# The gate and retention-value projections of a hybrid decoder block as twelve pairs of blocks in seven parts each, with h sums and gates kept in DRAM

## The chip, the cores and the metric

The kernel runs on one core of one Trainium2 chip. The metric is the device time of one execution in microseconds (us); less is better. Three runs of the kernel before gave a median of 1450.76 us (1450.04 to 1456.05).

## The reference, cut to what is computed

One decoder block for 1024 positions of width 1024, in float32. h is the RMS-normalised input; one matrix `w_in` projects it to everything the two branches need.

```python
h = rms_norm(x, g_mix)
q1, q2, k1, k2, va, qr, kr, vr, gr, gate_a, gate_r = split(h @ w_in)
a = diff_attention(q1, q2, k1, k2, va, lam)        # 4 heads, causal, ALiBi
a = _rms(a) * g_diff_sub * (1 - lam_init)
r = _rms(retention(qr, kr, vr)) * silu(gr)         # 4 heads, 8 chunks of 128 positions
merged = sigmoid(gate_a) * (a @ w_diff_proj) + sigmoid(gate_r) * (r @ w_ret_proj)
x = x + merged @ w_out
z = causal_dwconv(rms_norm(x, g_ffn) @ w_up)       # then silu(zg) * zu, @ w_down, a last RMS norm
```

The projections that the change rewrites are gr (512 columns of `w_in`), gate_a and gate_r (1024 each) and vr (512): 24 column blocks of 128.

## The kernel before, in words

Every fp32 product is made of three float32r matmuls: each operand is split into a high part (an ACT copy, `hi`) and a rest (a DVE subtraction, `lo`), and the kernel sums hi x hi, hi x lo and lo x hi (`product`, L200; `split`, L161; `weight`, L183). h lies transposed in SBUF as `hT`, eight pairs of 128x1024 tiles (tags `h0`, `h1`). SBUF tiles come from tags with a fixed number of slots (`BUFS`, L38), so a new tile waits until the slot's former tile is no longer read. PSUM has four tags, `g`, `x`, `b` and `r`, of two banks each while the branches run (L267).

The first part of `hybrid_block` runs, in the order of the text: va; normalisation of h; then for each of four heads `queries_keys` (L393: two `gemm` calls of 48 matmuls each) and `attention` (L417: eight query blocks, scores in bank `x`, an Exp, transposes in `b`, the product in `r`). After the last head come `retention_queries_keys` (L470, qr and kr) and `retention_gate` (L485, gr). `branch` (L510) scales and transposes the attention output into `aT`; `row_major` (L363) makes vr, with positions on the partitions, in matmuls of 256 columns. The retention loop (L547) works on chunk after chunk: scores `pst`, output `por`, transposed keys `pk`, state update `pu`. `gated` (L602) makes one gate block by a `gemm` over h (48 matmuls of 512 columns), a Sigmoid, and the projection of a branch (24 matmuls); it runs eight times for ga with the attention branch (`pspa`) and eight times for gt with the retention branch (`pspr`), with `branch` on the retention output between them.

The order of instructions in this part is fixed at build time by a planner, which goes by the priority of the text and by its own estimates of durations; each engine then executes its list in order. DMAs are issued from SP's queue, in a list of its own. The later part (`wo`, `up`, `wd`) is written differently: `seven_parts` (L796) and `up_step` (L986) compute products of 2x2 blocks in seven block products in place of eight (parts 1 to 7, with sums and differences of blocks), each a step of 12 matmuls per bank; `issue` (L713) emits the steps by hand, loads nine steps ahead, sums four, high parts three and rests two, under a manual schedule that keeps the text's order on PE, DVE, ACT and POOL.

## Time and profile before

| what | us |
|---|---|
| median of 3 runs | 1450.76 |
| lowest, highest | 1450.04, 1456.05 |
| the profiled execution, its own time | 1455.26 |
| its span, first to last instruction | 1453.5 |
| PE busy in it | 1393.8 (96%) |
| DVE busy | 969.0 (67%) |
| ACT busy | 658.9 (45%) |
| POOL busy | 171.6 (12%) |

Stages of the profiled execution, in us from the start of its span: normalisation and va to 68; attention with the products of q, k, qr, kr and the first gr blocks to 321; vr (316 to 368), retention (344 to 473) and ga with the attention branch (396 to 550); gt with the retention branch to 682; wo to 770; up to 1223; wd to 1440. A busy share says how long an engine had an instruction in work; whether its work set the end is read from who waited for whom in a stage.

### The profile page before, as it was taken

What the parts mean: (1) busy time and instruction counts of PE and PEld (TensorE: products, weight loads), DVE (VectorE), ACT (ScalarE), POOL (GpSimd) and SP (SyncE); (2) the same over time, 40 slices, a digit from 0 to 9 for tenths busy, and PEclk for the clock granted to TensorE, in tenths of its full rate; (3) what the DMA queues carried; (4) which work ended last, traced back from release to release, by engine and by line L of the source; (5) the groups of instructions that cost most, each with busy time, mean ns of one, the idle gap of its engine ahead of it and who ended that gap; (6) DMA issues with size and microseconds to landing.
All of it is one profiled execution on the core that took longest, in us unless ns stands there. A gap on an engine that the chain in (4) does not pass through costs nothing.

```text
span 1453.5 us, 18160 instructions
## 1 busy us (share of the span) xinstructions
PE 1393.8 (96%) x6776; PEld 1168.4 (80%) x6776; DVE 969.0 (67%) x1499; ACT 658.9 (45%) x1222; POOL 171.6 (12%) x127
## 2 busy tenths in 40 slices
PE   6899999999999999999988789999999999999996
PEld 6888888899888888888866468888888888788885
DVE  6746775552333315334978878988888899797876
ACT  6536565473222212113454355555555556454452
POOL 6621011000000000000000001111111112200000
PEclk9999999999999999999999889999999999999998
DMA  6310101000101111115224224433344365953233
GB/s 240 115 58 30 30 16 44 30 30 30 44 23 44 44 44 44 58 58 191 96 87 140 60 87 138 138 127 126 132 138 138 123 205 184 328 175 115 88 94 116
DMA packets 60472, 145.60 MB, mean 100 GB/s; under 512 B 6720, under 2 KB 9152, under 8 KB 60384
## 3 DMA queue, kind: packets, MB, share of 16 engines
q1 hardware_dynamic: 60192, 143.79, 29.8%
q8 instruction: 53, 0.87, 0.2%
q0 software_dynamic: 192, 0.66, 0.1%
q14 instruction: 35, 0.29, 0.1%
HBM read 115.84 MB, written 28.57 MB: 99 GB/s over the span
## 4 chain that ended last, share of the span: by engine, by line
PE 82%; DVE 8%; ACT 3%; issue 2%; DMA 2%; POOL 2%; SPq 0%; DVEq 0%; ACTq 0%; POOLq 0%
PE up L657 26%; PE wd L657 11%; PE psga L206 6%; PE psgt L206 6%; PE wo L657 4%; PE ps_vr L206 3%; PE psgr L206 3%; PE pspa L206 3%; PE pspr L206 3%; PE psk L206 3%; PE psq L206 3%; PE pss L431 2%; PE po L459 2%; PE pskr L206 2%; PE psqr L206 2%
## 5 line engine op out<-in xcount | busy, mean ns | idle before, releaser
L657 PE MATMUL up<-f,wf 128*128 128x512 f32 x1848 | 432.6, 395 | 18.2 <-ACT f L670 9.0
L657 PEld LDWEIGHTS up<-f,wf 128*128 128x128 f32 x1848 | 350.3, 190 | 99.9 <-ACT f L670 12.5
L657 PE MATMUL wd<-awd,wwd 128*128 128x512 f32 (+1 forms) x960 | 211.5, 382 | 2.1 <-DVE awd L664 2.1
L657 PEld LDWEIGHTS wd<-awd,wwd 128*128 128x128 f32 x960 | 175.3, 188 | 37.6 <-DVE awd L664 2.5
L657 PE MATMUL wo<-awo,wwo 128*128 128x512 f32 x336 | 80.8, 399 | 5.2 <-DVE awo L664 4.9
L657 PEld LDWEIGHTS wo<-awo,wwo 128*128 128x128 f32 x336 | 63.6, 191 | 21.7 <-DVE awo L664 7.3
L206 PE MATMUL psga<-hT,hi_ga 128*128 128x512 f32 x256 | 79.1, 391 | 0.3 <-ACT merged L605 0.3
L206 PE MATMUL psgt<-hT,hi_gt 128*128 128x512 f32 x256 | 78.1, 390 | 0.0
L1090 DVE SCALAR_TENSOR_TENSOR y<-zg,par,y 128x1022 f32<-128x1022 f32 (+1 forms) x44 | 58.6, 1333 | 5.0 <-ACT y L1087 5.0
L441 ACT ACTIVATE s<-s,row 128x512 f32<-128x512 f32 (+7 forms) x64 | 49.4, 773 | 23.4 <-DVE row L436 22.8
L664 POOL TENSOR_TENSOR t12g<-y 128x512 f32<-128x512 f32 x11 | 19.2, 1746 | 315.9 <-DVE y L1100 183.9
L667 DVE TENSOR_TENSOR zg<-zg,up 128x512 f32<-128x512 f32 x44 | 30.2, 686 | 39.2 <-PE up L657 38.4
L206 PEld LDWEIGHTS psga<-hT,hi_ga 128*128 128x128 f32 x256 | 48.0, 188 | 10.3 <-ACT merged L605 0.6
L1090 DVE SCALAR_TENSOR_TENSOR y<-zu,par,y 128x1022 f32<-128x1022 f32 (+1 forms) x44 | 56.1, 1276 | 0.0
L206 PEld LDWEIGHTS psgt<-hT,hi_gt 128*128 128x128 f32 x256 | 48.0, 188 | 9.8
L436 DVE CUSTOM_DVE_ANT_0 s<-pss,dist_t 128x512 f32<-128x512 f32 (+3 forms) x64 | 36.9, 588 | 27.0 <-PE pss L431 25.0
L670 ACT ACTIVATE zg<-up 128x512 f32<-128x512 f32 x44 | 26.3, 597 | 62.8 <-PE up L657 62.8
L664 DVE TENSOR_TENSOR awd<-act_in,awd 128x512 fp32r<-128x512 f32 x77 | 53.7, 697 | 0.0
L431 PE MATMUL pss<-k,q 128*128 128x512 f32 (+2 forms) x192 | 50.4, 370 | 2.4 <-DVE row L436 2.3
L206 PE MATMUL psga<-hT,lo_ga 128*128 128x512 f32 x128 | 50.2, 397 | 0.0
L164 DVE TENSOR_TENSOR lo_gt<-raw_gt,hi_gt 128x1024 fp32r<-128x1024 f32 x8 | 9.8, 1226 | 59.5 <-ACT hi_gt L163 59.5
L206 PE MATMUL psgt<-hT,lo_gt 128*128 128x512 f32 x128 | 48.8, 390 | 0.0
(311 smaller groups left out, 2814.9 us busy)
## 6 DMA issues: line engine op xcount, KB each, us to landing
act_in<-act SPq DMA_DIRECT2D x77, 256.0 KB, 2.9
act<-y SPq DMA_DIRECT2D x55, 256.0 KB, 2.1
raw_zg<-in_wall SPq DMA_DIRECT2D x22, 512.0 KB, 3.6
raw_zu<-in_wall SPq DMA_DIRECT2D x22, 512.0 KB, 4.2
x<-in_x SPq DMA_DIRECT2D x15, 512.0 KB, 8.4
act<-t12g SPq DMA_DIRECT2D x22, 256.0 KB, 2.0
wdu<-in_wall SPq DMA_DIRECT2D x22, 256.0 KB, 5.2
wdv<-in_wall SPq DMA_DIRECT2D x22, 256.0 KB, 4.7
```

The costliest lines, as they stand in the source:

```text
L164: engine.tensor_tensor(lo, src, hi.bitcast(F32), op=ALU.subtract)
L206: nc.tensor.matmul(ps, w, a, start=i == 0, stop=i == n - 1)
L431: nc.tensor.matmul(ps[:, : max(n, 256)], qs[m][:, i * P : (i + 1) * P], k[:, c : c + max(n, 256)], start=e == 0, stop=e == 1,)
L436: nc.vector.tensor_tensor_reduce(s[:, c : c + n], ps[:, :n], dst_t[:, S - width + c : S - width + c + n], SLOPES[h], low_, op0=ALU.add, op ...
L441: nc.scalar.activation(s[:, :width], s[:, :width], AF.Exp, bias=low_, scale=-1.0, accum_out=z[:, m : m + 1])
L459: nc.tensor.matmul(po, at[:, k * P : (k + 1) * P], va[h][:, kb, :], start=kb == 0, stop=kb == i)
L657: nc.tensor.matmul(ps[:, cols], w[:, x + at : x + at + P], a[:, y + cols.start : y + cols.stop], start=start and i == 0, stop=stop and i = ...
L664: engine.tensor_tensor(out, a, b, op=ALU.subtract)
L667: engine.tensor_tensor(out, a, b, op=ALU.add)
L670: nc.scalar.activation(out, a, AF.Copy)
L1090: nc.vector.scalar_tensor_tensor(y[side][:, n:], z[:, : S - n], t[:, j : j + 1], y[side][:, n:], op0=ALU.mult, op1=ALU.add)
```

## The change

- Columns of gr, ga, gt and vr are taken as 12 pairs of blocks. With the two halves of the positions and the two halves of the width a pair is a 2x2 block product, made in seven parts of 12 matmuls of 512 columns (`Pair`, on the `Step` and `issue` machinery that moves up from the later part).
- Sums of blocks of h (`h_sums`) are made on DVE in the middle of the attention stage and stored in DRAM; `h_side` loads them back in halves and splits them for parts 4 to 7. Part 5's lie over the second half of `hT[0..3]`.
- vr is made with columns on the partitions like the other pairs and transposed chunk by chunk.
- qr, kr (`retention_product`) and the finished gates go to DRAM (`spill`) and are loaded back when used (`loaded`). The decay of q is a DVE multiplication after the reload.
- The last head's attention is cut in three pieces with higher priority; steps 0 to 3 of the pairs stand between the pieces, all others after `branch` for the attention output.
- Retention runs after all pairs, with the inputs of chunk c+1 (`chunk_inputs`) ahead of chunk c, and the projection of the attention branch (`pspa`) follows it in the text.

```diff
-    for p in range(2):
-        halves(("vr", p), w_in, O_VR + p * 256)
+    for i in range(NH):
+        add(("vr", i), _unit_columns(w_in, np.arange(O_VR + i * P, O_VR + (i + 1) * P)))
...
+    def part(ps, ws, acts, start, stop, cols=slice(0, 512)):
+        n = 3 * len(ws)
+        i = 0
+        for (w, at), a in zip(ws, acts):
+            for x, y in ((0, 0), (0, 1), (1, 0)):
+                nc.tensor.matmul(
+                    ps[:, cols], w[:, x * 512 + at : x * 512 + at + P], a[y][:, cols],
+                    start=start and i == 0, stop=stop and i == n - 1, skip_group_check=True,
...
+    def issue(first=-LOAD, end=None):
+        n = len(steps)
+        for i in range(first, n if end is None else end):
+            for ahead, ops in (
+                (0, lambda s: s.first), (LOAD, lambda s: s.load), (SUMS, lambda s: s.sums), (HI, lambda s: [f.hi for f in s.forms]),
+                (LO, lambda s: [f.lo for f in s.forms]), (0, lambda s: s.pre + [s.mm] + s.post),
+            ):
...
+    def manual():
+        return tc.manual_schedule(engines={getattr(mybir.EngineType, n) for n in ("PE", "DVE", "Activation", "Pool")})
...
-        def row_major(name, dst, tags):
...
-        def attention(h, qs, ks):
-            oa.append(t4("vo", f"oa{h}", shape=(P, NST, DV)))
-            for i in (3, 7, 6, 5, 4, 2, 1, 0):
+        def attention(h, qs, ks, blocks=(3, 7, 6, 5, 4, 2, 1, 0)):
+            if len(oa) == h:
+                oa.append(t4("vo", f"oa{h}", shape=(P, NST, DV)))
...
-        def retention_queries_keys(p):
...
-        def retention_gate(h):
...
+        def spill(name, i, t):
+            spilled[name, i] = dram.tile([P, S], F32, name=f"{name}_saved{i}")
+            nc.sync.dma_start(out=spilled[name, i], in_=t)
+        def loaded(name, i, tag):
+            t = t4(tag, f"{name}{i}_in")
+            queue.last = nc.sync.dma_start(out=t, in_=spilled[name, i]).ins
+            return t
+        def retention_product(name, p):
+            t = t4("br", f"{name}{p}")
+            gemm((name, p), "g", f"{name}{p}", lambda cs, ps: copy(t[:, cs], ps), nc.gpsimd)
+            spill(name, p, t)
...
+        def h_sums():
+            for k in range(HK):
+                a, b = t4("vo", f"ta{k}"), t4("br", f"tb{k}")
+                for t, e in ((a, k), (b, k + HK)):
+                    plus(t, hT[0][e].bitcast(F32), hT[1][e].bitcast(F32))
+                b11, b12, b21, b22 = a[:, 0:512], a[:, 512:], b[:, 0:512], b[:, 512:]
+                sub(b11, b12, b11)
+                sub(b12, b22, b12)
+                sub(b22, b22, b11)
+                sub(b21, b21, b22)
+                t_saved.append([dram.tile([P, S], F32, name=f"t_saved{e}_{k}") for e in range(2)])
+                for t, d in zip((a, b), t_saved[k]):
+                    nc.sync.dma_start(out=d, in_=t)
+        h_sides = {(p, k): [t[k + q][:, cs] for t in hT] for p, q, cs in ((1, 0, first_half), (2, HK, first_half), (3, HK, second_half)) for k in range(HK)}
+        def h_side(p, k, tag=None):
+            if tag:
+                t = t4(tag, f"ht{p}_{k}", F32R)
+                hi, lo = t[:, 0:512], t[:, 512:]
+            else:
+                hi, lo = (t[k][:, second_half] for t in hT)
+            e, cs = {5: (0, first_half), 7: (0, second_half), 4: (1, first_half), 6: (1, second_half)}[p]
+            nc.sync.dma_start(out=lo.bitcast(F32), in_=t_saved[k][e][:, cs])
+            split(lo.bitcast(F32), hi, lo)
+            h_sides[p, k] = hi, lo
...
+        class Pair:
+            def __init__(self, i, name, e, func, done):
+                self.i, self.names, self.func, self.done = i, ((name, e), (name, e + 1)), func, done
+                self.label = f"{name}{e}"
+                self.tags = ("wraw", "wraw") if i % 2 == 0 else ("vo", "g")
+            def load(self, q):
+                t = t4(self.tags[q], f"raw{q}_{self.label}")
+                queue.load_unit(t, self.names[q])
+                if q == 0:
+                    self.a11, self.a12 = t[:, 0:512], t[:, 512:]
+                else:
+                    self.a21, self.a22 = t[:, 0:512], t[:, 512:]
...
+            def add(self, p):
+                side = {1: "a11", 2: "a12", 5: "a21", 6: "s2", 7: "a11", 3: "a12", 4: "a22"}[p]
+                w = weight_form(lambda: getattr(self, side), f"w{self.label}_{p}")
+                into_a = p in (1, 6, 7, 4)
+                def mm():
+                    if p == 1:
+                        self.a = psum("g", f"pa_{self.label}")
+                    if p in (2, 5):
+                        self.b = psum("x", f"pb{p}_{self.label}")
+                    part(
+                        self.a if into_a else self.b, [(w.t, k * P) for k in range(HK)],
+                        [h_sides[p, k] for k in range(HK)], p in (1, 2, 5), True,
+                    )
+                load, sums, post = [], [], []
+                if p == 1:
+                    load.append(partial(self.load, 0))
...
+                    def sums_5():
+                        sub(self.a11, self.a11, self.a21)
+                        self.s2 = t4("at", f"s2_{self.label}", shape=(P, 512))
+                        sub(self.s2, self.a22, self.a11)
+                        plus(self.a21, self.a21, self.a22)
...
+        for i, p in ((0, 1), (0, 2), (1, 1), (1, 2), (0, 5), (0, 6), (0, 3), (0, 7), (1, 5), (0, 4)):
+            pairs[i].add(p)
+        for i in range(1, len(pairs)):
+            for e, p in ((0, 6), (1, 1), (0, 3), (0, 7), (1, 2), (0, 4), (1, 5)):
+                if i + e < len(pairs):
+                    pairs[i + e].add(p)
         qk = queries_keys(0)
-        for h in range(NH):
+        for h in range(NH - 1):
             attention(h, *qk)
-            if h + 1 < NH:
-                qk = queries_keys(h + 1)
-            else:
-                for p in range(2):
-                    retention_queries_keys(p)
-                for e in range(2):
-                    retention_gate(e)
+            qk = queries_keys(h + 1)
+            if h == 1:
+                h_sums()
+        attention(3, *qk, (3, 7, 6))
+        level = tc.cur_priority
+        for name in ("qr", "kr"):
+            for p in range(2):
+                retention_product(name, p)
+        for k in range(HK):
+            h_side(5, k)
+        for p, tag in ((6, "br"), (7, "br")):
+            for k in range(HK):
+                h_side(p, k, tag)
+        def urgent():
+            return tc.high_priority(tc.cur_priority - level)
+        with urgent():
+            attention(3, *qk, (5, 4))
+        with manual():
+            issue(end=2)
+        with urgent():
+            attention(3, *qk, (2, 1, 0))
+        with manual():
+            issue(2, 4)
+        for k, tag in enumerate(("br", "c", "c", "c")):
+            h_side(4, k, tag)
         gd = one.tile([P, 1], F32, name="gd")
         nc.vector.tensor_scalar(gd, par[:, PAR_SUB : PAR_SUB + 1], 1.0 - LAM_INIT, None, op0=ALU.mult)
...
-        vr = [t4("vo", f"vr{i}", shape=(P, 2, 512)) for i in range(4)]
-        aT = branch(oa, ssq_a, lambda h, st: oa[h][:, st, :], "a", ("c", "c", "br", "s"), finish_a)
+        aT = branch(
+            oa, ssq_a, lambda h, st: oa[h][:, st, :], "a", (("vo", "c"), ("vo", "s"), ("vo", "s"), ("vo", "vo")), finish_a
+        )
+        with manual():
+            issue(4)
+        merged = [None] * KB
+        MERGED = ("br",) * 5 + ("s", "s", "vo")
+        merged[0] = loaded("ga", 0, MERGED[0])
+        rq, rk = ([loaded(name, p, "h1") for p in range(2)] for name in ("qr", "kr"))
         for p in range(2):
-            row_major(("vr", p), lambda st: vr[st // 2][:, st % 2, p * 256 : (p + 1) * 256], "gx")
+            q = rq[p].rearrange("p (c s) -> p c s", c=NST)
+            nc.vector.tensor_tensor(q, q, qd_c[:, p].broadcast_to([P, NST, P]), op=ALU.mult)
+        for j in range(1, 5):
+            merged[j] = loaded("ga", j, MERGED[j])
+        sgr = [loaded("gr", h, "h0") for h in range(NH)]
+        vr = []
         orr = []
         ssq_r = one.tile([P, NST * NH], F32, name="ssq_r")
-        state = None
         qz = t4("g", "qz", shape=(P, 2, 2, 2, P))
         nc.gpsimd.memset(qz, 0.0)
-        for c in range(NST):
+        heads = [(h, h // 2, slice((h % 2) * HD, (h % 2 + 1) * HD), slice(h * DV, (h + 1) * DV)) for h in range(NH)]
+        ready = {}
+        def chunk_inputs(c):
             cs = slice(c * P, (c + 1) * P)
             q = qz[:, c % 2]
             for p in range(2):
                 for e, rows in ((0, low), (1, top)):
                     nc.gpsimd.tensor_copy(q[rows, p, e, :], rq[p][rows, cs])
+            pv = psum("b", f"pv{c}")
+            for i in range(NH):
+                nc.tensor.transpose(pv[:, i * P : (i + 1) * P], vT[i][:, cs], ident)
+            if c % 2 == 0:
+                vr.append(t4("br", f"vr{c}", shape=(P, 2, 512)))
             v = vr[c // 2][:, c % 2, :]
-            heads = [(h, h // 2, slice((h % 2) * HD, (h % 2 + 1) * HD), slice(h * DV, (h + 1) * DV)) for h in range(NH)]
+            copy(v, pv)
             pst = psum("r", f"pst{c}")
             for p in range(2):
                 nc.tensor.matmul(
...
+            kd = None
+            if c + 1 < NST:
+                pk = psum("b", f"pk{c}")[:, 0:256]
+                for p in range(2):
+                    nc.tensor.transpose(pk[:, p * P : (p + 1) * P], rk[p][:, cs], ident)
+                kd = t4("kd", f"kd{c}", shape=(P, 256))
+                nc.vector.tensor_tensor(
+                    kd.rearrange("p (h d) -> p h d", h=NH), pk.rearrange("p (h d) -> p h d", h=NH),
+                    kd_c.broadcast_to([P, NH, HD]), op=ALU.mult,
+                )
+            ready[c] = q, v, sc, kd
...
+        def chunk(c, state):
+            q, v, sc, kd = ready.pop(c)
+            new = None
+            if kd is not None:
+                pu = psum("r", f"pu{c}")
+                for p in range(2):
+                    vs = slice(p * 256, (p + 1) * 256)
+                    nc.tensor.matmul(pu[:, vs], kd[:, p * P : (p + 1) * P], v[:, vs], start=True, stop=True)
+                new = t4("st", f"state{c}", shape=(P, 2, DV))
+                for h, p, rows, hs in heads:
+                    if c:
+                        nc.vector.scalar_tensor_tensor(
+                            new[rows, p, :], state[rows, p, :], math.exp(float(LOG_G[h]) * P), pu[rows, hs], op0=ALU.mult, op1=ALU.add
+                        )
+                    else:
+                        nc.vector.tensor_copy(new[rows, p, :], pu[rows, hs])
             po = psum("r", f"por{c}")
             for h, p, rows, hs in heads:
...
-            for h, p, rows, hs in heads:
-                if c:
-                    nc.vector.scalar_tensor_tensor(
-                        new[rows, p, :], state[rows, p, :], math.exp(float(LOG_G[h]) * P), pu[rows, hs], op0=ALU.mult, op1=ALU.add
-                    )
-                else:
-                    nc.vector.tensor_copy(new[rows, p, :], pu[rows, hs])
-            state = new
-        for h in range(2, NH):
-            retention_gate(h)
...
-        def gated(j, names, b, g):
-            gemm((names[0], j), "gx", f"{names[0]}{j}", lambda cs, ps: nc.scalar.activation(g[:, cs], ps, AF.Sigmoid))
-            w = weight((names[1], j))
+            return new
+        state = None
+        chunk_inputs(0)
+        for c in range(NST):
+            if c + 1 < NST:
+                chunk_inputs(c + 1)
+            state = chunk(c, state)
+        def gated(j, name, b, g):
+            w = weight((name, j))
             for c in range(2):
                 cs = slice(c * 512, (c + 1) * 512)
-                ps = psum("gx", f"ps{names[1]}{j}_{c}")
+                ps = psum("gx", f"ps{name}{j}_{c}")
                 channel_major(ps, w, lambda k: b[k], NH, c)
                 nc.vector.tensor_tensor(g[:, cs], g[:, cs], ps, op=ALU.mult)
-        merged = [t4("br" if j < 5 else "s" if j < 7 else "vo", f"merged{j}") for j in range(KB)]
-        for j in range(KB):
-            gated(j, ("ga", "pa"), aT, merged[j])
+        for j in (0, 1, 2, 3, 4, 7, 5, 6):
+            if merged[j] is None:
+                merged[j] = loaded("ga", j, MERGED[j])
+            gated(j, "pa", aT, merged[j])
...
-        rT = branch(orr, ssq_r, lambda h, st: orr[st // 2][:, st % 2 * NH + h, :], "r", ("c", "c", "br", "br"), finish_r)
-        HK = KB // 2
+        rT = branch(orr, ssq_r, lambda h, st: orr[st // 2][:, st % 2 * NH + h, :], "r", ("cc", "cc", ("br", "br"), ("br", "br")), finish_r)
         t12 = []
         for j in (0, 4, 1, 5, 2, 6, 3, 7):
-            g = t4("s", f"gr{j}")
-            gated(j, ("gt", "pr"), rT, g)
+            g = loaded("gt", j, "s")
+            gated(j, "pr", rT, g)
             nc.vector.tensor_tensor(merged[j], merged[j], g, op=ALU.add)
             if j >= HK:
                 b11, b12, b22 = merged[j - HK][:, 0:512], merged[j - HK][:, 512:], merged[j][:, 512:]
```

## Rows read from the trace of the kernel before

**Rows 1.** The page's head and its first part: span; engine, busy us (share of the span), instructions.

```profile
span 1453.5 us, 18160 instructions
PE 1393.8 (96%) x6776; PEld 1168.4 (80%) x6776; DVE 969.0 (67%) x1499; ACT 658.9 (45%) x1222; POOL 171.6 (12%) x127
```

**Rows 2.** Busy time by stage: stretch, its length, busy us and instructions of each engine, granted clock of PE, busy share of the DMA engines, GB/s.

```profile
94.80:285.00 190.20, 186.61 (x1020) 160.08 (x1019) 122.35 (x322) 108.80 (x256) 22.35 (x9) 0.99 0.09 29
285.00:321.30 36.30, 36.30 (x217) 32.07 (x216) 18.38 (x51) 25.23 (x51) 3.31 (x9) 1.00 0.14 43
...
396.00:473.00 77.00, 76.66 (x394) 65.55 (x392) 25.45 (x49) 16.43 (x55) 5.08 (x16) 1.00 0.12 35
...
550.00:682.00 132.00, 132.00 (x593) 109.38 (x592) 47.55 (x62) 28.95 (x44) 5.32 (x3) 1.00 0.20 66
```

**Rows 3.** What PE waited for from 60 to 690 us: us in total, times, longest.

```profile
PE pss L431 <- DVE row L436: 2.3, 3, 1.2
PE psq L206 <- POOL lo_q L164: 2.1, 1, 2.1
```

**Rows 4.** Groups of PE instructions from 280 to 700 us: count | busy us, mean ns of one | idle before. The mean is a latency, since matmuls overlap. A weight's high part takes part in two of the three matmuls of a product and its rest in one, so a lo row has half the count of its hi row.

```profile
L206 PE MATMUL psga<-hT,hi_ga 128*128 128x512 f32 x256 | 79.1, 391 | 0.3 <-ACT merged L605 0.3
L206 PE MATMUL psgt<-hT,hi_gt 128*128 128x512 f32 x256 | 78.1, 390 | 0.0
L206 PE MATMUL psga<-hT,lo_ga 128*128 128x512 f32 x128 | 50.2, 397 | 0.0
...
L206 PE MATMUL ps_vr<-hi_vr,hT 128*128 128x256 f32 x256 | 47.6, 285 | 0.0
L206 PE MATMUL psgr<-hT,hi_gr 128*128 128x512 f32 x128 | 40.2, 393 | 0.0
L206 PE MATMUL pspa<-a,hi_pa 128*128 128x512 f32 x128 | 39.9, 391 | 0.0
...
L206 PE MATMUL ps_vr<-lo_vr,hT 128*128 128x256 f32 x128 | 36.2, 285 | 0.0
```

**Rows 5.** The chain of work in order of time: start, us, instructions in an unbroken run.

```profile
344.96 23.03 PE ps_vr L206 x192
...
584.63 10.88 PE psgt L206 x48
```

**Rows 6.** PE in order of time: start, us to the end of the last, instructions.

```profile
326.68 1.04 PE L526 MATMUL pta<-cst,oa 128*128 128x128 f32 x8
327.47 0.48 PE L206 MATMUL ps_vr<-hi_vr,hT 128*128 128x256 f32 x2
```

**Rows 7.** Groups of DVE and ACT instructions from 60 to 800 us, shapes apart: count | busy us, mean ns of one | idle before.

```profile
L164 DVE TENSOR_TENSOR lo_ga<-raw_ga,hi_ga 128x1024 fp32r<-128x1024 f32 x8 | 9.8, 1225 | 43.5 <-ACT hi_ga L163 43.5
L163 ACT ACTIVATE hi_ga<-raw_ga 128x1024 fp32r<-128x1024 f32 x8 | 8.5, 1061 | 31.8 <-PE psga L206 25.9 <-PE psgr L206 5.9
L664 DVE TENSOR_TENSOR awo<-merged,awo 128x512 fp32r<-128x512 f32 x16 | 10.9, 682 | 0.0
L667 DVE TENSOR_TENSOR x<-x,wo 128x512 f32<-128x512 f32 x24 | 16.3, 684 | 9.3 <-PE wo L657 9.3
L670 ACT ACTIVATE awo<-merged 128x512 fp32r<-128x512 f32 x16 | 9.9, 617 | 0.0
L605 ACT ACTIVATE gr<-psgt 128x512 f32<-128x512 f32 x16 | 9.4, 589 | 40.8 <-PE psgt L206 40.8
```

**Rows 8.** The same view as rows 2, for the up stage.

```profile
873.00:1222.00 349.00, 348.31 (x1537) 288.07 (x1537) 310.64 (x352) 187.94 (x280) 65.49 (x39) 1.00 0.43 142
```

**Rows 9.** DMA issues: tile, queue, count, KB each, median us from issue to landing.

```profile
raw_ga<-in_wall SPq DMA_DIRECT2D x8, 512.0 KB, 3.3
...
x_saved<-x SPq DMA_DIRECT2D x16, 256.0 KB, 2.0
```

**Rows 10.** The retention loop: all its `por` matmuls of one kind (first and last start), and one chunk in order of time (start, us, engine, instructions).

```profile
L564 PE MATMUL por<-vr,rs x64: 270/275/276, 367.8 to 472.7; 128*128 128x128 f32 x64
...
428.51 0.38 PE L564 MATMUL por<-vr,rs 128*128 128x128 f32 x2
...
430.29 0.38 PE L578 MATMUL pk<-cst,rk 128*128 128x128 f32 x2
...
436.89 1.02 PE L587 MATMUL pu<-vr,kd 128*128 128x256 f32 x4
437.75 1.03 PE L557 MATMUL pst<-qz,rk 128*128 128x256 f32 x4
...
440.22 0.38 PE L564 MATMUL por<-vr,rs 128*128 128x128 f32 x2
...
444.06 0.42 DVE L580 TENSOR_TENSOR kd<-pk,cst 128x256 f32<-128x256 f32 x1
...
448.75 1.02 PE L587 MATMUL pu<-vr,kd 128*128 128x256 f32 x4
```

**Rows 11.** Groups of DVE and ACT instructions from 60 to 800 us, on the way from the last retention chunk to the retention branch's operand: count | busy us, mean ns of one | idle before.

```profile
L573 ACT ACTIVATE jkr<-or 128x128 f32<-128x128 f32 x32 | 9.5, 299 | 26.1 <-DVE or L570 26.1
L573 ACT ACTIVATION_READ_ACCUMULATOR jkr<-or 128x1 f32 x32 | 6.0, 188 | 0.0
L518 DVE TENSOR_TENSOR or<-or,rstd_r 128x1024 f32<-128x1024 f32 x4 | 4.6, 1219 | 0.0
L619 DVE TENSOR_TENSOR y<-ptr,sgr 128x512 f32<-128x512 f32 x8 | 5.3, 684 | 5.3 <-PE ptr L526 5.3
```

**Rows 12.** The same view as rows 2, for the stretch with the longest holes of PE.

```profile
800.00:840.00 40.00, 28.08 (x85) 18.83 (x85) 31.39 (x50) 15.89 (x28) 0.00 (x0) 0.79 0.18 53
```

More of the change, by code (lines that the diff above doesn't have):

```diff
@@ new lines, in hybrid_block, with weight_form, __init__, step @@
+    n_forms = [0]
+    def weight_form(src, name):
+        n_forms[0] += 1
+        return Form(("whi", "wlo")[n_forms[0] % 2], src, name)
+    class Step:
+        def __init__(self, label, mm, load=(), sums=(), forms=(), post=()):
+            self.label, self.mm, self.load, self.sums, self.forms = label, mm, list(load), list(sums), list(forms)
+            self.first, self.pre, self.post = [], [], list(post)
+    LOAD, SUMS, HI, LO = 9, 4, 3, 2
+    steps, index, behind = [], {}, []
+    def step(label, *args, **kwargs):
+        index[label] = len(steps)
+        steps.append(Step(label, *args, **kwargs))
@@ new lines, in spread @@
+    def spread(first, last, ops):
+        i, j = (index[x] if isinstance(x, tuple) else x for x in (first, last))
+        for n, op in enumerate(ops):
+            steps[i + n * (j + 1 - i) // len(ops)].post.append(op)
+    def issue(first=-LOAD, end=None):
[5 more added lines that the diff above has]
+            ):
+                if 0 <= i + ahead < n:
+                    for op in ops(steps[i + ahead]):
+                        op()
@@ L707, in spread @@
-    def spread(first, last, ops):
-        i, j = (index[x] if isinstance(x, tuple) else x for x in (first, last))
-        for n, op in enumerate(ops):
-            steps[i + n * (j + 1 - i) // len(ops)].post.append(op)
-    def issue():
-        n = len(steps)
-        for i in range(-LOAD, n):
-            for ahead, ops in (
-                (0, lambda s: s.first), (LOAD, lambda s: s.load), (SUMS, lambda s: s.sums), (HI, lambda s: [f.hi for f in s.forms]),
-                (LO, lambda s: [f.lo for f in s.forms]), (0, lambda s: s.pre + [s.mm] + s.post),
-            ):
-                if 0 <= i + ahead < n:
-                    for op in ops(steps[i + ahead]):
-                        op()
@@ L1260, in hybrid_block @@
     at(("wd", 4, "d", 1, 3), row0, column1, *rest0, row1, *rest1)
-    with tc.manual_schedule(engines={getattr(mybir.EngineType, n) for n in ("PE", "DVE", "Activation", "Pool")}):
+    with manual():
         issue()
```

172 lines of the change are left out of this document (82 added, 90 removed).

## The prediction

> **What bounds the kernel now.** I read the busy shares first: PE is busy for 1393.8 of 1453.5 us, DVE for 969.0 [rows 1]. A share over the whole span hides stages, so I cut the span by stage next. Wherever the change works PE has almost no hole: 186.6 of 190.2 us in the attention stage, all of 36.3, 76.7 of 77.0, all of 132.0, at a granted clock of 0.99 to 1.00, while DVE is busy for at most 64% of any of these [rows 2]. The list of what PE waited for between 60 and 690 us confirms it: the largest entry is 2.3 us [rows 3]. So in this region time falls only if PE has less to do, and rises if PE finds something not ready.
>
> **Matmuls.** Removed: ga 256 + 128, gt as many, gr half as many, 960 matmuls of 512 columns; vr 256 + 128, 384 of 256 columns [rows 4]. The chain gives paces, which the means do not, since those are latencies: 48 in 10.88 us, 0.2267 each; 192 of the narrow kind in 23.03 us, 0.120 each [rows 5]. So 960 x 0.2267 = 217.6 and 384 x 0.120 = 46.1, together 263.7 us. Added: 12 pairs x 7 parts x 12 = 1008 x 0.2267 = 228.5 us. vr now comes with columns on the partitions and needs 32 transposes; eight transposes hold PE from 326.68 to 327.47, 0.10 each [rows 6], so 3.2 us. Net on PE: 263.7 - 228.5 - 3.2 = 32.0 us less, on the path.
>
> The Trainium skill (TensorE: Matmul & The Clock Gate, section Back-to-back issue gap) gives a warm spacing of N / 2.4 GHz plus 2.5 ns, 216 ns at 512 columns and 109 ns at 256. By it the first difference would be an estimated 31.4 instead of 35.2 us; the rows are slower, most so for the narrow matmuls, and the sum goes by the rows.
>
> **Operands of the pairs.** A pair needs seven rests (DVE 0.682), four sums of weight blocks and three additions from PSUM (0.684 each): 14 x 0.683 = 9.6 us of DVE. ACT has seven high parts (0.617), three copies from PSUM (0.589), a function over 1024 columns (nearest row 1.061) and two over 512 (0.589): 8.3 us [rows 7]. PE works 84 x 0.2267 = 19.04 us on a pair, so both hide. The up stage is the same machinery with more on DVE, 310.6 of 349.0 us, and PE is busy for 348.3 of them [rows 8]. Steady pairs: 1 us of holes, between 0 and 4. POOL gets nothing new; its rests of q, k, qr and kr stay.
>
> **h sums and sides.** Per k two additions over 1024 columns (1.225) and four over 512 (0.684): 5.2, four times 20.7 us of DVE [rows 7] in a stage where DVE is free for 68 of 190 us [rows 2]. The 16 sides cost 16 x 0.617 = 9.9 us of ACT and 16 x 0.682 = 10.9 us of DVE, mostly late in that stage. Attention has the higher priority there, so I count nothing on the path; if DVE had no room they would cost their 20.7 us.
>
> **DMAs.** 72 more on SP's queue: 8 stores of sums, 16 half loads, 24 spills, 24 reloads, about 34 MB, on 9 to 15% busy DMA engines [rows 2]. A load of 512 KB lands in 3.3 us, a store of 256 KB in 2.0 [rows 9]. A spill waits for ACT's last pass over its block, and the next weight loads queue behind it; but a load is issued nine steps, 9 x 2.72 = 24.5 us, ahead, so the queue may slip by several landings. Nothing on the path.
>
> **Start of the pairs.** Attention needs other work in PE's gaps. Before, after q, k, qr and kr this was gr: 96 matmuls, 21.8 us. Now steps 0 to 3 give 48 matmuls, 10.9 us, and steps 4 and 5 another 5.4 if part 5's sides are there, which are written over hT after the last qr and kr product. Then a second wait: pair 1's second tile takes the one slot of tag `g`, which holds the distance table until the last score. The load (3.3), three sums (2.1) and a form (1.3) make 6.7 us, and on DVE the rests of the next steps stand behind those sums in the text's order. The hole is 0 if steps 4 and 5 and the transposes of `aT` (32, 3.2 us) cover it, and 10.9 + 6.7 = 17.6 us if nothing does. I take 5: nearer to nothing, as PE waited 2.3 us for scores in the whole stage [rows 3], so the planned order had slack.
>
> **Retention and the attention branch.** Before, retention had ga beside it and was never short of cover. Now there is `pspa` alone: 128 + 64 matmuls [rows 4], 43.5 us. Of its own work a chunk has eight output matmuls (428.51 to 430.29, 1.8 us), state update and scores (0.86 each, the distance of their starts), two key transposes and four new ones (0.6): 4.1 us [rows 6, 10]. So PE has 8 x 4.1 + 43.5 = 76.3 us, and 3.2 us of transposes for the retention branch. A chunk took 11.7 us from output to output (428.51 to 440.22), 4.3 of them between the end of `kd` and `pu`, which nothing needed [rows 10]: the plan was stretched because other work was there. With the next chunk's inputs ahead, scores, keys and `kd` leave the chain, so a chunk lies between 4.1 and 11.7 us; I take 7.5, as the part of the old chain that stays is about half of it. Behind the last chunk come a copy of about 0.7, four squares (0.299 + 0.188 each, 2.0), root and reciprocal (an estimated 2), scalings (2 x 1.22 for the first piece), a transpose, and eight pieces of 0.684 + 0.682: some 19 us to the last piece, 9 to the first [rows 7, 11]. The chain is 8 x 7.5 + 19 = 79 against 79.5 us of PE work. Not all of the cover will fall where it is wanted: I take a hole of 5 us, from 0 to 20.
>
> **Reloads and wo.** q and k of retention come back into slots that free some 10 us before the last step, four loads of 3.3 us: 1 us, up to 5. The retention projection runs without gt's products, so behind the last slot of `wraw` wo's weights have two projections, 48 matmuls and 10.9 us, in place of a gate and a projection, 16.3: 2 us, up to 6.
>
> **Sum.** 32.0 - (1 + 5 + 5 + 1 + 2) = 18 us. The profiled execution took 1455.3 us, 1.8 more than its span [rows 1], and would take 1437; it lies 4.5 above the median of the runs, so I put the median at 1450.8 - 18 = 1433 us. A measurement of this kernel can tell about 0.5%, 7.3 us, from no change.
>
> **Rivals.**
> - All hidden (chance 0.20): every hole near zero, as PE had none before; there were also 3.6 us of holes in the attention stage to lose. 1417 to 1424 us. For it: the free shares of DVE and ACT [rows 2]. Against: the cover shrinks at two places.
> - Holes dearer than their length (0.11). From 800 to 840 us PE was idle for 11.9 us, the granted clock fell to 0.79 (part of the time at 1.2 GHz), and 85 matmuls were done, 19.3 us at 0.2267: 20.7 us lost for 11.9 of holes, 1.74 times [rows 12]. My 14 us would then cost 24 and the gain be 8: 1443 us. Against: short scattered holes left the clock at 0.99 [rows 2]. The Trainium skill (TensorE: Matmul & The Clock Gate, Part 1) says that the throttled clock is the default and activity lifts it; the rows agree.
> - No gain (0.09): sums and sides crowd DVE in the attention stage, so that its scores come late: 20.7 us beside the 9 of the other holes, 32 - 30 = 2: 1449 us. For it: slots of `vo` and `br` are scarce there. Against: 68 us of DVE were free.
> - Slower (0.08): retention keeps its old step. It decides from T = 11.4 us per chunk: the hole is 8 T + 19 - 79.5, and 32 - 9 + 7.3 = 30.3 of it make the kernel 0.5% slower. At the 11.7 seen it is 33 us: 1461 us; at the mean of old starts, (472.7 - 367.8) / 7 = 15.0, it is 59.5: 1487 us [rows 10]. For it: the planner's order may again be far looser than the durations. Against: the inputs come one chunk ahead, and the planner stretched only where it had cover.
>
> The forecast has the remaining 0.52, from 1424 to 1442 us.
>
> **Numbers.** Faster: 0.52 less 0.02 for its edge, 0.20, and half of the dear holes, 0.06, with 0.02 of the third: 0.78. Slower 0.08; within 0.5% the other 0.14. The range reaches from all hidden, 1417, to the no-gain case with its edge, 1450; it leaves out the slower case and little else.
>
> **What would show it.** Right: some 84 matmuls per 19 us over 11 pairs with PE never idle; the retention branch's operand ready less than 5 us after the last `pspa`; wo starting 15 to 20 us earlier than 682. Wrong: PE waits for a side, for `raw` of pair 1 or for pair forms (start); PE idle for over 10 us between the last chunk and the first `pspr` (retention); `pss` waiting for DVE in heads 2 and 3 (sums); a granted clock under 0.95 between 300 and 680 us. If the region from 95 to 660 is dense and the gain still misses, the pace of the pairs was not 0.2267.

## The result and the profile after

The changed kernel took 1470.7 us (median; 1468.3 to 1476.1) beside 1450.6 for the kernel before: ratio 1.0135, 95% interval 1.0098 to 1.0173. It is slower by 20 us where 18 less were forecast; the range ended at 1450. The profiled execution took 1469.6 us. The page of the changed kernel, to be held against [rows 1]:

```profile
span 1467.7 us, 18058 instructions
...
PE 1380.4 (94%) x6472; PEld 1140.4 (78%) x6472; DVE 1067.6 (73%) x1673; ACT 702.4 (48%) x1312; POOL 175.8 (12%) x127
```

PE does less, as planned, and yet the span is longer: it must idle, or run slowly, somewhere. The windows of the changed kernel (columns as in [rows 2]) say where. First the whole region of the change, then the steady pairs, `wo`, `up`, `wd`, then seven slices of 10 us:

```profile
60.00:690.00 630.00, 592.49 (x2890) 492.12 (x2889) 367.45 (x729) 276.34 (x599) 54.17 (x54) 0.96 0.26 91
...
360.00:540.00 180.00, 180.00 (x796) 148.99 (x795) 85.90 (x133) 75.73 (x124) 0.00 (x0) 1.00 0.33 110
698.00:786.00 88.00, 81.14 (x345) 64.53 (x344) 74.61 (x119) 42.66 (x79) 6.50 (x1) 0.98 0.34 122
786.00:1239.00 453.00, 434.80 (x1858) 352.81 (x1859) 392.88 (x472) 237.96 (x365) 67.71 (x40) 0.97 0.39 130
1239.00:1454.00 215.00, 212.91 (x976) 177.04 (x974) 173.82 (x275) 102.86 (x186) 10.25 (x4) 1.00 0.47 159
...
180.00:190.00 10.00, 6.09 (x20) 3.85 (x21) 10.00 (x21) 3.88 (x9) 2.59 (x1) 0.71 0.44 159
190.00:200.00 10.00, 7.27 (x47) 6.01 (x46) 10.00 (x30) 6.32 (x20) 0.00 (x0) 0.95 0.26 106
200.00:210.00 10.00, 7.53 (x29) 6.30 (x30) 8.20 (x22) 3.94 (x13) 0.00 (x0) 0.66 0.26 105
330.00:340.00 10.00, 2.27 (x10) 1.79 (x10) 7.77 (x12) 3.67 (x8) 0.00 (x0) 0.72 0.16 52
340.00:350.00 10.00, 8.88 (x34) 6.95 (x34) 4.51 (x7) 5.25 (x10) 0.00 (x0) 0.59 0.01 2
...
630.00:640.00 10.00, 7.20 (x53) 6.13 (x51) 3.91 (x8) 3.58 (x21) 1.17 (x4) 1.00 0.01 4
640.00:650.00 10.00, 4.75 (x16) 2.94 (x17) 7.54 (x10) 3.48 (x9) 0.00 (x0) 0.58 0.00 1
```

From 60 to 690 us PE idles 37.5 of 630 us; by the same view it idled 7.8 in the kernel before, at a clock of 0.99. The pairs are dense, and the later stages last as long as before: `wo` starts at 697.5 in place of 682.4 us, and the end is later by about as much. So the loss lies ahead of `wo`, mostly in three holes: 176 to 210 (A), 329 to 350 (B), 623 to 650 us (C). What PE waited for in the changed kernel (us in total, times, longest), beside [rows 3]:

```profile
PE pss L502 <- DVE row L507: 9.2, 10, 2.3
PE ptr L754 <- DVE or L746: 6.8, 4, 5.4
PE pta L754 <- DVE oa L746: 5.7, 1, 5.7
PE pat L525 <- DVE s L517: 3.9, 4, 1.9
PE pta L754 <- DVE a L762: 2.7, 2, 2.0
...
PE por L841 <- DVE state L834: 2.1, 2, 1.2
```

Every line names VectorE, none a transfer (VectorE and ScalarE themselves waited 1.0 to 1.5 us for transfers at 323 to 327 us, while PE had work). Each hole in order of time (start, us, engine, instruction, idle before).

**Hole A.** The h sums (`ta`, `tb`) stand between the attention's VectorE instructions. One of them took 2.31 us, where the same form took 0.68 at 192.25, beside a GpSimd instruction, and PE's longest wait for scores (2.33 us) ends behind it. The q evictions of head 3 start at 200.65 us (174.21 in the kernel before), so bank `g` is full and no q or k matmul can fill:

```profile
180.15 2.59 POOL L164 TENSOR_TENSOR lo_qr<-raw_qr,hi_qr 128x1024 fp32r<-128x1024 f32 x1 [14.09 <-ACT hi_qr L163]
180.97 2.31 DVE L285 TENSOR_TENSOR tb<-tb,ta 128x512 f32<-128x512 f32 x1
183.94 3.03 PE L502 MATMUL pss<-k,q 128*128 128x512 f32 x6 [2.33 <-DVE row L507]
...
185.62 1.22 DVE L288 TENSOR_TENSOR ta<-hT,hT 128x1024 f32<-128x1024 f32 x1
...
186.76 1.14 DVE L517 SCALAR_TENSOR_TENSOR s<-s,row,s 128x896 f32<-128x896 f32 x1
...
188.04 1.73 PE L525 MATMUL pat<-cst,s 128*128 128x128 f32 x7 [1.07 <-DVE s L517]
...
200.65 0.69 DVE L472 SCALAR_TENSOR_TENSOR q<-psq,q 64x512 fp32r<-64x512 f32 x1
...
202.40 1.30 PE L525 MATMUL pat<-cst,s 128*128 128x128 f32 x5 [1.89 <-DVE s L517]
...
206.42 1.20 PE L206 MATMUL psk<-hT,hi_k 128*128 128x512 f32 x2
```

**Hole B.** After the last output of attention PE's list has the branch's transposes (`pta`) ahead of the next pair step, and PE waits there 5.70 us for the branch's scale; a copy of the pairs (`z_gr`, 0.59 us) stands on ScalarE behind five evictions of the branch, and the next pair step needs its bank. The first line is the first sum from the tile in slot `g` that the prediction named:

```profile
326.00 0.69 DVE L285 TENSOR_TENSOR raw_gr<-raw_gr,raw_gr 128x512 f32<-128x512 f32 x1 [1.52 <-DMA raw_gr<-in_wall]
...
329.28 0.83 PE L530 MATMUL po<-va,at 128*128 128x128 f32 x6
...
334.44 4.63 DVE L746 TENSOR_TENSOR oa<-oa,rstd_a 128x1024 f32<-128x1024 f32 x4
335.81 1.94 PE L754 MATMUL pta<-cst,oa 128*128 128x128 f32 x8 [5.70 <-DVE oa L746]
...
343.61 0.69 ACT L761 ACTIVATE a<-pta,gd 128x512 fp32r<-128x512 f32 x1 [1.14 <-PE pta L754]
344.20 0.59 ACT L291 ACTIVATE z_gr<-pb_gr 128x512 f32<-128x512 f32 x1
...
344.84 4.53 PE L276 MATMUL pb_gr<-hT,wgr 128*128 128x512 f32 x12 [0.41 <-ACT z_gr L291]
```

**Hole C.** `pspa` starts at 558.1 us, 16 us ahead of the first output of retention (574.1), and its last matmul at 626.1, while the last chunk's outputs run to 638.5. Behind them stands the chain to the retention operand, with nothing to cover it:

```profile
638.09 0.39 PE L843 MATMUL por<-state,qz 128*128 128x128 f32 x2
...
638.52 0.69 DVE L847 COPY or<-por 128x512 f32<-128x512 f32 x1 [1.09 <-PE por L843]
...
640.60 1.28 ACT L742 ACT_TABLE_LOAD   x1
...
642.63 4.63 DVE L746 TENSOR_TENSOR or<-or,rstd_r 128x1024 f32<-128x1024 f32 x4
643.91 0.69 PE L754 MATMUL ptr<-cst,or 128*128 128x128 f32 x2 [5.44 <-DVE or L746]
...
648.69 1.20 PE L206 MATMUL pspr<-r,hi_pr 128*128 128x512 f32 x2
```

**The account** of the two profiled executions. The changed kernel starts `wo` 15.1 us later, though its first q product comes 3.0 us earlier (65.9 in place of 68.9 us): in the first 60 us the kernel before lost 3.0 us to a lower clock (0.94), the changed one none. So the stretch from the first q product to `wo` takes 18.1 us longer. In it stand 32.0 us less work, 36.7 - 6.1 = 30.6 more idle time, and 13.0 more from the clock (PE's busy time x (1 - granted clock), summed over slices of 1 us from 60 us on: 16.2 against 3.2). That makes +11.6; 6.5 us were not found in rows. By place, more than in the kernel before (idle + clock): hole A, 170 to 220 us, 7.9 + 3.8; hole B with the stretch ahead of it, 280 to 360, 13.3 + 4.6; hole C, 625 to 670, 9.3 + 3.3.

### The profile page after: what moved, and what is told of

Same layout as the page of the kernel before. It is cut to its first block, busy times and chain, and to the rows that moved or that the text cites. A ratio compares the mean times of both kernels' runs of the same rounds, so it can differ in the third digit from the quotient of the medians.

```text
span 1467.7 us, 18058 instructions
## 1 busy us (share of the span) xinstructions
PE 1380.4 (94%) x6472; PEld 1140.4 (78%) x6472; DVE 1067.6 (73%) x1673; ACT 702.4 (48%) x1312; POOL 175.8 (12%) x127
## 4 chain that ended last, share of the span: by engine, by line
PE 79%; DVE 10%; ACT 4%; issue 2%; POOL 2%; DMA 2%; SPq 0%; DVEq 0%; ACTq 0%; POOLq 0%
PE up L276 27%; PE wd L276 14%; PE wo L276 4%; PE psk L206 3%; PE pa_gt L276 3%; PE pa_ga L276 3%; PE pspr L206 3%; PE pspa L206 3%; PE psq L206 3%; PE pb_gt L276 2%; PE pb_ga L276 2%; PE po L530 2%; PE pss L502 2%; PE psqr L206 1%; PE pa_vr L276 1%
## 5 line engine op out<-in xcount | busy, mean ns | idle before, releaser
L276 PEld LDWEIGHTS up<-f,wf 128*128 128x128 f32 x1848 | 351.5, 191 | 100.3 <-ACT f L291 12.5
L502 PE MATMUL pss<-k,q 128*128 128x512 f32 (+2 forms) x192 | 54.4, 380 | 9.5 <-DVE row L507 9.2
L507 DVE CUSTOM_DVE_ANT_0 s<-pss,dist_t 128x512 f32<-128x512 f32 (+3 forms) x64 | 37.1, 586 | 25.5 <-PE pss L502 24.1
L291 ACT ACTIVATE awd<-act_in 128x512 fp32r<-128x512 f32 x77 | 47.4, 616 | 0.2 <-DVE wf L285 0.2
L502 PEld LDWEIGHTS pss<-k,q 128*128 128x128 f32 x192 | 32.5, 195 | 17.7 <-DVE row L507 14.4
L291 ACT ACTIVATE zu<-up 128x512 f32<-128x512 f32 x44 | 26.3, 597 | 41.8 <-PE up L276 41.6
L206 PE MATMUL psq<-hT,hi_q 128*128 128x512 f32 x128 | 42.6, 409 | 2.1 <-ACT hi_q L163 1.7
L291 ACT ACTIVATE wwd<-wdv 128x512 fp32r<-128x512 f32 x33 | 20.9, 632 | 46.0 <-PE wd L276 37.0
L206 PE MATMUL pspa<-a,hi_pa 128*128 128x512 f32 x128 | 42.5, 406 | 0.0
L206 PE MATMUL psk<-hT,hi_k 128*128 128x512 f32 x128 | 41.8, 401 | 0.0
```

Source lines behind the costliest of these rows:

```text
L206: nc.tensor.matmul(ps, w, a, start=i == 0, stop=i == n - 1)
L276: nc.tensor.matmul(ps[:, cols], w[:, x * 512 + at : x * 512 + at + P], a[y][:, cols], start=start and i == 0, stop=stop and i == n - 1, sk ...
L291: nc.scalar.activation(out, a, AF.Copy)
L502: nc.tensor.matmul(ps[:, : max(n, 256)], qs[m][:, i * P : (i + 1) * P], k[:, c : c + max(n, 256)], start=e == 0, stop=e == 1,)
L507: nc.vector.tensor_tensor_reduce(s[:, c : c + n], ps[:, :n], dst_t[:, S - width + c : S - width + c + n], SLOPES[h], low_, op0=ALU.add, op ...
```

## The experiments

Times stand against the changed kernel's 1470.7 us; the kernel before took 1451 to 1452 us beside them. Each of the first four undoes one hole.

**e1: no sums (A).**

```diff
-                a, b = t4("vo", f"ta{k}"), t4("br", f"tb{k}")
-                ... two additions, four subtractions
-                for t, d in zip((a, b), t_saved[k]):
-                    nc.sync.dma_start(out=d, in_=t)
+                for e, d in zip((k, k + HK), t_saved[k]):
+                    nc.sync.dma_start(out=d, in_=hT[0][e].bitcast(F32))
```

> The h sums' work on VectorE and the slots that they hold are left out: parts 4 to 7 of every pair read plain columns of h in place of the sums (every transfer, matmul and other instruction stays). Theory (three local holes, each with TensorE's lower clock behind it; this is the first, at 176 to 210 us, VectorE full with the sums while the q evictions of head 3 wait): TensorE's idle time at 170 to 220 us falls from about 9 to about 2 us, the granted clock there goes from about .78 to .95 or more, and the time falls by 12 to 17 us against the changed kernel, to 1454 to 1459 us. Rival (the holes only take turns: what is done earlier before 210 us is waited for later, at the reloads of h or the attention's inputs): under 4 us, 1467 us or more. Rival (the loss is in the traffic of the sums through DRAM, which stays): no change.

1455.3 us, 15.4 less. In the slice from 180 to 190 us PE was busy for 7.66 at a clock of 1.00 and the next two had no idle time. The sums cost 15 us through VectorE or through their slots, not through DRAM.

**e2: sums one head later (A).** The call of `h_sums` moves from `h == 1` to `h == 2`.

> The h sums are traced one head later, so that the attention of head 2 and the q and k products of head 3 come ahead of them in the planned order. Theory (VectorE's order and the slots at 170 to 210 us make the first hole): the sums land over a longer stretch, some 200 to 260 us, the hole at 176 to 210 us shrinks to 3 us or less, and the time falls by 8 to 15 us, to 1456 to 1463 us. Rival (VectorE has no room anywhere between 60 and 285 us): the hole moves with the sums to 210 to 280 us and the time stays within 3 us of the changed kernel's 1470.7 us.

1458.2 us, 12.5 less. The old place has only the idle time that the kernel before had; a smaller hole came with the sums to their new place:

```profile
180.00:190.00 10.00, 8.12 (x50) 7.37 (x49) 7.91 (x28) 6.55 (x19) 2.38 (x1) 0.83 0.18 52
220.00:230.00 10.00, 10.00 (x62) 8.38 (x60) 9.93 (x21) 4.61 (x11) 2.80 (x1) 1.00 0.39 156
230.00:240.00 10.00, 6.38 (x28) 5.68 (x28) 9.91 (x27) 4.91 (x14) 0.08 (x1) 0.67 0.34 121
```

**e4: 24 pair steps ahead of the branch (B).**

```diff
+        with manual():
+            issue(4, 24)
         aT = branch(
...
         with manual():
-            issue(4)
+            issue(24)
```

> The first 24 steps of the pairs are given their places ahead of the attention branch's evictions in the planned order, where the changed kernel gives 4. Theory (the second hole, 329 to 345 us: the pairs' copies on ScalarE and VectorE stand behind the branch's evictions and scales): the pair matmuls fill the stretch, TensorE idles 3 us or less at 329 to 350 us where it idled about 9, the granted clock stays above .9 there, and the time falls by 8 to 14 us, to 1457 to 1463 us. Rival (what is late there is the data of the first pairs, raw tiles and sums read back from DRAM): the idle time stays where it is and the time falls by less than 3 us.

1459.3 us, 11.4 less. In e4 the same copy comes at 328.90 us, and pair steps cover the branch's chain:

```profile
326.63 0.69 DVE L285 TENSOR_TENSOR raw_gr<-raw_gr,raw_gr 128x512 f32<-128x512 f32 x1 [2.06 <-DMA raw_gr<-in_wall]
...
328.90 0.60 ACT L291 ACTIVATE z_gr<-pb_gr 128x512 f32<-128x512 f32 x1
...
331.42 2.60 PE L276 MATMUL pb_gr<-hT,wgr 128*128 128x512 f32 x10 [0.77 <-DVE wgr L285]
```

From 330 to 340 us PE is busy for 9.23 in place of 2.27, at a clock of 1.00. From 325 to 360 us it idles 2.7 us in place of 8.9. The tile in slot `g` came no earlier (its first sum starts at 326.63 us, 326.00 in the changed kernel), so the data of the first pairs were there in time: the order was what was late.

**e5: two products kept back (C).** In the planned order the `pa` products 5 and 6 get a place behind the last output of retention (`last_po` is that matmul; the dependency orders the plan only, without a semaphore).

```diff
-            gated(j, "pa", aT, merged[j])
+            gated(j, "pa", aT, merged[j], last_po[0] if j in (5, 6) else None)
```

> Of the branch projection's gated products that run beside the retention, the last two (j = 5 and 6) wait for the retention's last output matmul. Theory (the third hole, 629 to 649 us: all of them are used up at 626 us, ahead of the last chunks and of the chain of ScalarE and VectorE to the retention operand): the two products, some 7 us of matmuls, fall into that chain, TensorE idles 3 us or less at 638 to 649 us, and the time falls by 6 to 12 us, to 1459 to 1465 us. Rival (the chunks run at their own latency and those products were needed between them): the hole of 7 us opens between the chunks instead, the last output matmul keeps its distance to the first, and the time stays within 3 us of 1470.7 us. Rival (the pause before TensorE's clock falls is what costs, not the idle time itself): the gain is 4 us or less though the idle time falls.

1463.2 us, 7.5 less. From 630 to 640 us PE is never idle and from 640 to 650 for 0.5 us. The distance from the first to the last output is 55.0 us (577.0 to 632.0) in place of 63.9, so the chunks did not need those products. From the first output to the start of `wo` the traces have 116.1 us in place of 123.4: 7.3 less, with 5.0 less idle time and hole C's 3.3 of low clock gone.

**e3: sums on GpSimd (A).** Additions and subtractions of `h_sums` get `nc.gpsimd`.

> The h sums are added and subtracted on GpSimd in place of VectorE, at the same place of the order and in the same slots. Theory (VectorE's time makes the first hole): VectorE is no longer full at 176 to 210 us, TensorE idles 4 us or less at 170 to 220 us where it idled 10.3, and the time falls by 7 to 15 us against the changed kernel's 1470.7 us, less what the slots, held for longer by the slower engine, give back. Rival (the sums' four tiles in the slots of the branch's and the v columns' tag hold up the q and k products): the hole stays or grows, GpSimd having the tiles for longer, and the time is 1468 us or more.

1470.2 us: no gain. That looks like the rival, the slots (the q evictions of head 3 come at 202.8 to 219.0 us), but the trace of e3 gives a second possible reason. VectorE's `L517` (two operands from SBUF) took 3.06 us for 768 columns, where the same form took 1.00 at 192.85 us in the changed kernel; `L507`, which reads one from PSUM, kept its 0.68:

```profile
187.41 2.33 POOL L288 TENSOR_TENSOR ta<-hT,hT 128x1024 f32<-128x1024 f32 x1
187.49 3.06 DVE L517 SCALAR_TENSOR_TENSOR s<-s,row,s 128x768 f32<-128x768 f32 x1
189.82 1.87 POOL L285 TENSOR_TENSOR ta<-ta 128x512 f32<-128x512 f32 x1
190.48 0.68 DVE L507 CUSTOM_DVE_ANT_0 s<-pss,dist_t 128x512 f32<-128x512 f32 x1
```

VectorE was blocked while GpSimd worked, so e3 does not tell VectorE's time from the slots. The next two do.

**e7 and e8: each half alone (A).** e7 keeps the sums' VectorE instructions but not their slots (one tile of `vo` takes all results); e8 keeps the slots, filled by a transfer, without the instructions.

```diff
+            junk = t4("vo", "junk")                                    # e7
+            half = junk[:, 0:512]
...
+                for e in (k, k + HK):
+                    plus(junk, hT[0][e].bitcast(F32), hT[1][e].bitcast(F32))
+                for i in range(4):
+                    sub(half, junk[:, 512:], half)
...
-                    plus(t, hT[0][e].bitcast(F32), hT[1][e].bitcast(F32))
+                    nc.sync.dma_start(out=t, in_=hT[0][e].bitcast(F32))  # e8, and the four sub() left out
```

> First hole, VectorE's part alone: the sums' 24 VectorE instructions stay at their place, in the same shapes, but all write one tile of the v columns' tag and nothing is made of them; no slot of the branch tag (br) is taken; the stores take plain columns of h. Parts 4 to 7 of the pairs read plain columns of h. Theory a (VectorE's time makes the hole): 1466 us or more, the hole stays as in the changed kernel. Theory b (the br slots make it: the q tiles of head 3 come late, so that bank g stays full and no q or k matmul can fill): the q evictions come at 170 to 195 us as in the version without the sums, the hole is mostly gone, and the time is 1455 to 1461 us. In between, 1461 to 1466: both take part.

> First hole, the slots alone: the same eight tiles in the same slots at the same place, filled by a transfer of plain columns of h and stored, with no VectorE instruction. Parts 4 to 7 of the pairs read plain columns of h. Theory a (VectorE's time): the hole is gone, 1453 to 1459 us. Theory b (the slots): q evictions at 195 us or later, the hole stays, 1463 us or more.

e7 1466.5, e8 1454.6 us. The slice from 180 to 190 us, of e7:

```profile
180.00:190.00 10.00, 6.70 (x36) 5.77 (x36) 9.94 (x21) 3.48 (x8) 1.29 (x1) 0.66 0.19 55
```

and of e8:

```profile
180.00:190.00 10.00, 8.32 (x56) 6.89 (x54) 7.81 (x25) 8.09 (x19) 2.37 (x1) 1.00 0.66 246
```

VectorE's instructions make most of the hole. In e7 the q evictions come at 171.3 to 197.9 us, as in the kernel before (174.2 to 197.6), and still PE idles 7.2 us from 170 to 220 us (10.3 in the changed kernel, 2.4 before). So the late q evictions are not the main cause. The slots alone only delay: in e8 the q evictions come at 186.5 to 195.0 us, and PE idles 2.6 us there, about as before. With the sums, at most some 4 us (1470.7 - 1466.5) are theirs.

**e6: matmuls that fill (C, the price of the clock).**

```diff
+        for c in range(2):
+            ps = psum("gx", f"again_{c}")
+            channel_major(ps, weight(("pa", 6)), lambda k: aT[k], NH, c, last_po[0])
```

> The changed kernel, with 24 matmuls (5.4 us at full clock) that repeat the product of weight block pa 6, result unused, and with that block's load and split once more; they wait for the retention's last output matmul, so that they fall into the third hole (638 to 649 us). Nothing of the useful work moves. Theory (a hole costs its length and the lower clock behind it): the fill keeps the clock at 1 through 640 to 660 us (it was .74), and the time falls by 3 to 5 us though the useful matmuls wait as long as before. Rival (only the length counts): the time stays, or rises by what the fill delays the transposes, 0 to 5 us.

1469.3 us, inside the changed kernel's spread: nothing decided. The fill covered 640.1 to 645.8 us; the transposes behind it, 0.7 us apart, and the eviction let the clock fall 5 us later instead:

```profile
640.00:645.00 5.00, 5.00 (x26) 4.14 (x25) 1.55 (x3) 4.00 (x16) 0.00 (x0) 1.00 0.00 2
645.00:650.00 5.00, 2.78 (x12) 1.25 (x10) 5.00 (x6) 0.63 (x1) 0.00 (x0) 0.92 0.61 210
650.00:655.00 5.00, 4.01 (x15) 3.52 (x16) 4.39 (x8) 2.19 (x4) 0.00 (x0) 0.50 0.31 105
```

**The three together, and variants.** `c_all` is e2 + e4 + e5.

> The three changes together: h sums one head later, 24 pair steps ahead of the branch's evictions, the last two gated products behind the last retention output. Theory (three separate holes): the gains add, 12.5 + 11.4 + 7.6 = 31.5 us, 1439 us, faster than the kernel before (1451.1 us) by 12 us; the net matmul saving of 32 us is then cut by some 20 us of idle time and low clock that stay (220 to 240, 280 to 320, 610 to 630 us). Rival (the holes take turns, one gives way to the next): 1447 us or more.

1440.2 us; against the kernel before 0.9919 (0.9900 to 0.9938). The gains add: 31.5 forecast, 30.5 measured. The region of the change in `c_all`:

```profile
60.00:690.00 630.00, 609.65 (x2999) 509.33 (x2998) 390.29 (x766) 288.79 (x624) 60.45 (x55) 0.98 0.30 102
```

20.4 us idle, 17.2 less than in the changed kernel. `c_spread` makes half of the sums behind head 1, half behind head 2.

> As the three changes together, but the h sums in two halves, one behind the attention of head 1 and one behind that of head 2. Theory (VectorE has a limited room at each head): the remaining hole at 220 to 240 us, 3.6 us of idle time and 3 us of low clock, is divided or gone, and the time is 1433 to 1437 us, 2 to 6 us under the version with the sums in one piece. Rival (each half opens a hole of its own, with the clock's fall behind each): as the other or up to 5 us slower.

1447.8 us, the rival, and 7.6 us over `c_all` where it allowed 5: each half opened a hole (PE busy 6.28 from 180 to 190 us, 7.61 from 220 to 230). `c_later` puts them behind the first blocks of head 3.

> As the version with all three changes (1440.2 us), but the h sums are traced still later, behind the first groups of head 3's attention. Theory (the 3.5 us of idle time and the low clock at 230 to 240 us come from the sums going ahead of that attention's VectorE work): the hole goes and the time falls by 2 to 6 us, to 1434 to 1438 us. Rival (the sums then land too late for the high sides of the pairs): a hole at 285 to 320 us, 1442 us or more.

1442.7 us: the hole at 230 us shrank to 2.2 us, while 290 to 320 us grew from 3.4 to 5.5; within 0.5% of `c_all`. `c_halves` spreads the held products:

```diff
-                channel_major(ps, w, lambda k: b[k], NH, c, after)
+                n = n_half[0]
+                n_half[0] += 1
+                at = None if name == "pr" else None if n < 2 else 7 if n > 11 else (n - 2) * 7 // 10
+                channel_major(ps, w, lambda k: b[k], NH, c, None if at is None else last_po[at])
```

> As the version with all three changes (1440.2 us), but the branch projection's gated products are held in halves of 12 matmuls: two free, ten spread behind the outputs of chunks 0 to 6, four behind the last. Theory (the 3.6 us between the last two chunks that no product fills are a matter of where the fill stands): they shrink to 1 us or less and the time falls by 2 to 4 us, to 1436 to 1438 us. Rival (early chunks then wait, since the fill is held from them): 1440 us or more.

1436.2 us, against before 0.9875 (0.9859 to 0.9892). Between the chunks PE idles 0.9 us from 600 to 610 us, where it was 2.55 in `c_all`. The runs of the two versions overlap (1435.0 to 1442.3, 1437.1 to 1444.6), but the traces bear the 4 us out: from the first q product to `wo` `c_halves` takes 601.1 us (68.9 to 670.0), `c_all` 605.1 (64.9 to 670.0), and from retention's first output to the first `pspr` 65.6 in place of 68.5. This is the best version run, faster than both kernels.

## Why the prediction was wrong

Three steps failed: the h sums, put at nothing, the start of the pairs and the retention, put at 5 us each. The forecast had 14 us of holes in all; the traces have 30.6 of idle time and 13.0 of low clock more than before.

- **Matmuls (32.0 us net): right, as far as rows show.** 796 matmuls in 180 us are 0.226 each, and `c_halves` shows that half of the saving can be had. The 6.5 us that the account does not find leave room for an error in it.
- **Operands of the pairs, DMAs, reloads: right.** No idle time from 360 to 540 us with VectorE at 48%; no transfer among PE's waits. (The DMA share in [rows 2] reaches 20%, not 15; nothing hung on it.)
- **wo (2 us taken): nothing.** The stage lasts 88.5 us (697.5 to 786), as before (682.4 to 771).
- **h sums, "nothing on the path": the worst step, 15.4 us by e1.** Two reasons fell. "Attention has the higher priority there" is false in the text's order: the sums are traced ahead of head 2's attention. And "68 of 190 us free" was a mean over 190 us, while the sums (20.7 us forecast, 22.2 measured) came within 160 to 207 us, and VectorE was busy for 10.0 of 10 us in two slices of it. The bound of 20.7 was the near one. The rival "no gain" named this mechanism but kept the other holes at 9 us.
- **Start of the pairs, 5 us: too small, 11.4 by e4, and the mechanism was another.** The waits named (the slot of `g`, part 5's sides) were not the bound: in e4 the tile in `g` came no earlier, and the hole shrank from 8.9 to 2.7 us. The branch's transposes stood ahead of the pair steps in PE's list, and pair copies and forms behind the branch's evictions in ScalarE's and VectorE's, while PE's other work was used up.
- **Retention, 5 us: too small.** e5 won back 7.5, and `c_halves` some 4 more. A chunk took 9.1 us on the mean ((638.0 - 574.1) / 7), but 5.3 where no product stood beside it (629.4 to 634.7): T = 7.5 was not the fault, nor did the old step return; the chain to the first piece, put at 9 us, took 10.2. The planner spent the cover early, from 558.1 us on, and those 10.2 us from the last output to the first `pspr` stood bare. The sum of chain and work said that it would just fit, and nothing in it said when the cover runs.
- **Holes dearer than their length: it happened too.** If the 32.0 hold, the changed kernel lost 18.1 + 32.0 = 50.1 us from the first q product to `wo` for 30.6 us of added idle time, 1.64 times, near the 1.74 of [rows 12]; 13.0 of the other 19.5 are low clock by the slices. Undoing a hole gave more than its idle time: e4 11.4 us for 5.6 us less of it ahead of `wo`, e5 7.5 for 5.0. The factor was at hand, the length of the holes was not. e6 failed to isolate it, so the clock's share rests on rows alone.

With the three holes repaired, 12.6 us more idle time than before remain in `c_all` (20.4 against 7.8), and 5.6 of low clock (8.8 against 3.2): 230 to 240, 290 to 310, 590 to 610 us. What would remove the one at 230 was not found.

## What to carry to other kernels

An engine's free time is a budget of the 10 or 20 us in which the new work falls, not of the stage: ask what the planned order puts ahead of what. Work that fills gaps has to be kept for the gap that has no other cover, usually the chain behind the last iteration; a total that fits says nothing of that. When PE falls from dense to gappy, price each hole at more than its length (1.6 to 1.7 times here).

## What the runs showed of the hardware

- VectorE instructions with two operands in SBUF wait for a running GpSimd tensor_tensor: 3.06 in place of 1.00 us (e3), about the end of GpSimd's instruction plus its own time (187.41 + 2.33 = 189.74; 190.55 - 189.74 = 0.81), and 2.31 in place of 0.68 in the changed kernel (180.97 us, beside GpSimd's instruction from 180.15 to 182.74). The instruction with one operand in PSUM was not touched. The Trainium skill (SBUF — State Buffer, section "SBUF: two separate sides") describes an exclusive lock between the two engines that a VectorE instruction with two SBUF inputs meets; the trace agrees. GpSimd itself took 2.33 us for an addition that VectorE does in 1.22.
- The granted clock fell to 0.71 and 0.66 in slices of hole A in which PE was busy for 6.1 and 7.5 of 10 us and no single wait was over 2.33 us; after hole C it was still 0.81 from 650 to 655 us with PE never idle.
